# The rotary steps of a grouped attention: another DMA queue, later due times, a ranked read-out, and a wider last attention

## The chip, the cores and the metric

The kernel runs on one core of a Trainium2 chip. The metric is the device time of one execution in microseconds, as the median of three runs. Before the change it is 1803.03 us (1802.46 to 1805.33).

## The reference, cut to what matters

An encoder of two layers on 512 tokens plus 16 meta tokens (T = 528), width 2048, float32. Layer 0 is grouped-query attention, layer 1 is gated linear attention. The change touches layer 0 alone:

```
proj = rmsnorm(h) @ w_in                    # q: 16 heads x 128, k, v: 8 x 128, gate: 2048
q = axial_rope(rmsnorm(q, q_norm))          # per head; likewise k
x1, x2 = split(x, 2)                        # inside each half of 64 rows
rotate(x) = concat(x1*cos - x2*sin, x2*cos + x1*sin)
o = softmax(q k^T * 128**-0.5) v            # one k/v head serves two q heads
y = (o * silu(gate)) @ w_out
```

## The kernel before, in words

Every float32 operand is split into a high part and the rest (`split`, L128: a cast on ACT, a subtraction on DVE), and each product is three matmuls on PE. A projection (`project`, L156) computes 128 output columns for all tokens in two halves of 264. It walks 16 blocks of the contraction, so it has 2 x 16 x 3 = 96 matmuls. Its weights come in two units of 512 KB on SP's queue (`wraw`, two buffers) and are split into `whi` and `wlo` (three buffers).

Attention runs in eight groups g, each with one k head and two q heads. While PE attends in group g (`attention`, L656: nine query tiles, each with scores, a softmax on DVE and ACT, transposes, and then the product with v), it also projects k, q, q and v for group g+1 (`qkv`, L565, and `values`, L539). Nothing else fills PE in that time. In the last group, g = 7, it projects the gates 13, 14 and 15 instead; after that comes the output projection (`group`, L746).

The order of emission is kept by a planner. `Clock` counts planned microseconds: each three matmuls of a projection advance it by 3 x 271/2400 = 0.339, so a projection is 10.84. `clk.after(dt, fn)` emits `fn` when the count reaches its due time, and `clk.drive` steps through a generator whose yields are such times. `SLOTS[g]` is the planned distance of two query tiles. From the emitted program each engine's order of instructions is then fixed when the program is built: of the instructions whose inputs that builder expects to be there, the earliest in the program goes first, and an instruction inside `tc.high_priority(400)` counts as 400 places earlier. Work of a later program place can so come ahead of its place where the builder expects an engine to be free. On the chip each engine then runs its list strictly in order.

A rotation (`rope`, L290) is run for each of the 3 x 8 projected k and q tiles. ACT writes the scaled projection `qw` and its square `sq` (L286, L287). Four DMAs of 32 rows each copy `qw` to `qs` with neighbouring blocks of 32 rows exchanged (L294). `sq` is split into `sh` and `sl`. POOL multiplies `qw` by cos and `qs` by sin (L299, L300). At two due times after the projection, `sums` runs for the two halves: PE adds the squares over the 128 rows by a product with ones into the PSUM tile `ssq` (L304, L305), and DVE reads it out into `f` (L306). That PSUM tile comes from the pool `ps_o`, which has one buffer, and the product with v (`weighted`, L645, matmuls from L650) uses the same buffer. So PE can start the second `sums`, or a product with v, only after DVE's read-out of the `sums` before it. At a later due time `late` computes the reciprocal root on ACT (L133, L134), adds `qs` to `qw` (L310), multiplies by the root (L311) and splits the result into the q or k tiles.

For group 0 there is no projection ahead: `first_group` (L574) starts the three rotations 4.2 planned us apart and then waits before the first attention tile; meanwhile PE projects for group 1.

Of the kernel before, what the change touches and what calls it, by code (L numbers as in the profile page):

```python
# [14 lines left out]
ALU = mybir.AluOpType  # L15
# [4 lines left out]
P = 128  # L20
# [12 lines left out]
G_HEADS = 4  # L33
SCALE = 128 ** -0.5
AHEAD = 400
SLOTS = (3.0, 3.5, 3.8, 3.8, 3.8, 3.8, 3.8, 2.6)


class Clock:
# [43 lines left out]
def hybrid_encoder(  # L83
# [5 lines left out]
    nc = tc.nc  # L89
    V, A, G, PE = nc.vector, nc.scalar, nc.gpsimd, nc.tensor  # L90
    clk = Clock()
# [27 lines left out]
    def col(i):  # L119
        return cols[:, i:i + 1]  # L120
# [7 lines left out]
    def split(hi, lo, src):  # L128
        A.copy(hi, src)  # L129
        V.tensor_tensor(lo, src, hi.bitcast(F32), op=ALU.subtract)  # L130

    def rsqrt_inplace(t):
        A.activation(t, t, AF.Ln)  # L133
        A.activation(t, t, AF.Exp, scale=-0.5)  # L134
# [21 lines left out]
    def project(src, c0, parts, evac, last_k=None, ws=None):  # L156

        ws = ws or [weights(src[:, k0:k0 + 8, c0:c0 + P]) for k0 in (0, 8)]
        for a, b in parts:
            ps = ps_p.tile([P, 512], F32, tag="pp", name="pp")[:, :b - a]  # L160
            for k in range(KT):
                wh, wl = ws[k // 8]
                three(ps, wh[:, k % 8], wl[:, k % 8], k, a, b, k == 0, k == KT - 1)
                clk.step(3 * (b - a + 7) / 2400)
                if last_k and (a, b) == parts[-1]:
                    last_k(k)
            evac(ps, a, b)
# [109 lines left out]
    erow = c0.tile([P, T], F32, name="erow")  # L277
    rcol = c0.tile([P, 5], F32, name="rcol")
    def take(wcol):

        qws.append(qws.pop(0))
        qw = qws[-1]
        sq = wk.tile([P, T], F32, tag="sq", name="sq")

        def evac(ps, a, b):
            A.activation(qw[:, a:b], ps, AF.Copy, scale=wcol)  # L286
            A.activation(sq[:, a:b], ps, AF.Square)  # L287
        return qw, sq, evac

    def rope(qw, sq, outs, steps):  # L290
        qs = wk.tile([P, T], F32, tag="qs", name="qs")
        for b in range(4):
            s = b ^ 1
            nc.sync.dma_start(out=qs[b * 32:b * 32 + 32, :], in_=qw[s * 32:s * 32 + 32, :])  # L294
        sh = wk.tile([P, T], F32R, tag="sh", name="sh", bufs=1)
        sl = wk.tile([P, T], F32R, tag="sl", name="sl", bufs=1)
        split(sh, sl, sq)
        f = sq
        G.tensor_tensor(qw, qw, cos, op=ALU.mult)  # L299
        G.tensor_tensor(qs, qs, sin, op=ALU.mult)  # L300

        def sums(a, b):
            ps = ps_o.tile([P, 512], F32, tag="o", name="ssq")[:, :b - a]
            PE.matmul(ps, ones_r, sh[:, a:b], start=True, stop=False)  # L304
            PE.matmul(ps, ones_r, sl[:, a:b], start=False, stop=True)  # L305
            V.scalar_tensor_tensor(f[:, a:b], ps, 1.0 / P, erow[:, a:b], op0=ALU.mult, op1=ALU.add)  # L306

        def late():
            rsqrt_inplace(f)
            V.tensor_tensor(qw, qw, qs, op=ALU.add)  # L310
            V.tensor_tensor(qw, qw, f, op=ALU.mult)  # L311
            for hi, lo, a, b in outs:
                split(hi, lo, qw[:, a:b])
        for step, part in zip(steps, HALVES):
            clk.after(step, lambda part=part: sums(*part))
        clk.after(6.5, late)

    def qk_tiles(p, n):
        kh, kl = [p.tile([P, T], F32R, name=f"k{w}{n}") for w in "hl"]
# [59 lines left out]
    for i, (si, off) in enumerate(((0, 0), (1, 0), (1, P))):  # L379
        for j, (a, b) in enumerate(HALVES):  # L380
            n = 2 * i + j
            if n < 3:
                ps = ps_p.tile([P, 512], F32, tag="pp", name="pp")
            else:
                ps = ps_g.tile([P, 512], F32, name=f"g{n}")
            ps = ps[:, :b - a]
# [152 lines left out]
    def values(g):  # L539
        vh = wa.tile([P, 4, P], F32R, tag="vh", name="vh")  # L540
        vl = wa.tile([P, 4, P], F32R, tag="vl", name="vl")
        vm = vm_bufs[g % 2]
        if g:
            project(w_in0, 3072 + g * P, HALVES, lambda ps, a, b: A.copy(vt[:, a:b], ps))

        def late():
            ps = ps_t.tile([P, 512], F32, tag="t", name="vps")
            for t in range(4):
                PE.transpose(ps[:, t * P:(t + 1) * P], vt[:, t * P:(t + 1) * P], ident)
            for t in range(4):  # L550
                pst = ps[:, t * P:(t + 1) * P]
                A.activation(vh[:, t, :], pst, AF.Copy, scale=rcol[:, t:t + 1])
                V.scalar_tensor_tensor(vl[:, t, :], pst, rcol[:, t:t + 1], vh[:, t, :].bitcast(F32),
                                       op0=ALU.mult, op1=ALU.subtract)
            pm = ps_t.tile([P, 512], F32, tag="t", name="vpm")[:META, :P]
            PE.transpose(pm, vt[:, SEQ:T], ident)
            rm = rcol[:META, 4:5]
            A.activation(vm[0:META], pm, AF.Copy, scale=rm)
            A.activation(vm[64:64 + META], pm, AF.Copy, scale=rm)
            V.scalar_tensor_tensor(vm[32:32 + META], pm, rm, vm[0:META].bitcast(F32),  # L560
                                   op0=ALU.mult, op1=ALU.subtract)
        clk.after(1.2 if g else 2.0, late)
        return vh, vl, vm

    def qkv(g):  # L565
        qk, outs = qks[g % 2]
        vv = values(g) if g == 1 else None
        for i, c in enumerate((2048 + g * P, 2 * g * P, (2 * g + 1) * P)):
            qw, sq, evac = take(col(KN if i == 0 else QN))
            project(w_in0, c, HALVES, evac)  # L570
            rope(qw, sq, outs[i], (4.4, 5.6))
        return qk, vv or values(g)

    def first_group():  # L574
        for i in range(3):
            sq = wk.tile([P, T], F32, tag="sq", name="sq")
            A.activation(sq, qws[i], AF.Square)
            A.activation(qws[i], qws[i], AF.Copy, scale=col(QN if i else KN))
            rope(qws[i], sq, qks[0][1][i], (2.6, 3.9))
            yield 4.2 if i < 2 else 7.5  # L580

    def stored_gates(hs, held):

        grs = [wa.tile([P, T], F32, tag="gr", name="gr") for _ in hs]
        for gr, h in zip(grs, hs):
            nc.sync.dma_start(out=gr, in_=g_d[h])
        yield 6.0
        for gr, h in zip(grs, hs):
            yield 5.0
            V.tensor_tensor(gr, gr, rrow, op=ALU.mult)  # L590
            gs = silu(gr)
            yield 4.0
            og = held[h % 2]
            V.tensor_tensor(og, og, gs, op=ALU.mult)
            nc.gpsimd.dma_start(out=og_d[h], in_=og)
# [7 lines left out]
    def gate(h, last_k=None):  # L603
        gr = wa.tile([P, T], F32, tag="gr", name="gr", bufs=2)
        project(w_in0, 4096 + h * P, HALVES,
                lambda ps, a, b: V.tensor_tensor(gr[:, a:b], ps, rrow[:, a:b], op=ALU.mult), last_k)
        return silu(gr)
# [79 lines left out]
    def o_tiles():  # L687
        return [wa.tile([P, T], F32, tag="o", name="o_sb", bufs=4) for _ in range(2)]
# [3 lines left out]
    for g in range(KV):  # L692
        o_sb = o_tiles()
        att = attention(qk, vv, o_sb, SLOTS[g])
        lead = first_group() if g == 0 else iter([6.5] if g == 1 else [])
        att = clk.drive(chain(lead, att))
        gates = [] if g == 0 else [2 * g - 2, 2 * g - 1]
        stored = clk.drive(stored_gates([h for h in gates if h < 13], held))
        if g + 1 < KV:
            nxt = qkv(g + 1)  # L700
        for h in gates:
            if h < 13:
                continue
            gs = gate(h)
            og = held[h % 2]
            V.tensor_tensor(og, og, gs, op=ALU.mult)
            nc.gpsimd.dma_start(out=og_d[h], in_=og)
        if g + 1 < KV:
            clk.finish(att, stored)
            qk, vv = nxt  # L710
            held = o_sb
# [28 lines left out]
    for m in range(2):  # L740
        for j, (a, b) in enumerate(HALVES):
            ps = (ps_t.tile([P, 512], F32, tag="t", name="po") if m and j else
                  ps_p.tile([P, 512], F32, tag="pp", name="pp"))[:, :b - a]
# [75 lines left out]
    for i in range(2):  # L819
        for a, b in HALVES:  # L820
            ps = ps_g.tile([P, 512], F32, name=f"g{i}{a}")[:, :b - a]
# [109 lines left out]
    for a, b in HALVES:  # L931
        ps = ps_t.tile([P, 512], F32, tag="t", name="lrf")[:64, :b - a]
# [481 lines left out]
```

## Time and profile before

| | |
|---|---|
| median of three runs | 1803.03 us |
| profiled execution, its own time | 1801.33 us |
| its span, first to last instruction | 1799.6 us |
| mean granted TensorE clock | 0.997 |
| PE busy (matmuls) | 1758.1 us, 98% |
| DVE busy | 1128.4 us, 63% |
| ACT busy | 951.3 us, 53% |
| POOL busy | 208.3 us, 12% |

Busy times of PE are those of pipelined matmuls, so a gap counts only once the last matmul in flight has ended. DMA-issuing instructions are not counted as busy. The attention of layer 0 lies between about 205 and 757 us.

### The profile page before, as it was taken

The page shows a single profiled execution, that of the slowest core. Times are in us where ns is not written, and L with a number is a line of the kernel's source. Part 1 is how long each engine was busy: PE and PEld are TensorE (multiplying, and loading weights), DVE is VectorE, ACT ScalarE, POOL GpSimd, SP SyncE. Part 2 cuts the span into 40 slices and gives each one's busy share as a digit, 9 for nine tenths or more (in the row PEclk, how much of TensorE's full clock was granted, in tenths as well). Part 3 has the DMA queues.
Part 4 walks back from the last instruction along what each step waited for, and adds up shares of the span by engine and source line. Part 5 has one row for each costly group of instructions (what it writes and reads, how often), then busy time and mean ns, then how long its engine had stood idle before and what let it go on. Part 6 is the DMA issues. An engine that isn't in the chain of part 4 may idle for free.

```text
span 1799.6 us, 31638 instructions
## 1 busy us (share of the span) xinstructions
PE 1758.1 (98%) x12591; PEld 1654.9 (92%) x12591; DVE 1128.4 (63%) x1904; ACT 951.3 (53%) x1909; POOL 208.3 (12%) x270
## 2 busy tenths in 40 slices
PE   8999899999999999999999999999999999999998
PEld 8999899999999999999999899988898989888886
DVE  5877687666666666641238787667585765764224
ACT  5543465555565555543338544477685765863221
POOL 3000212111211111121111101110000100000000
PEclk9999999999999999999999999999999999999999
DMA  8444433233232323243336344343232332345333
GB/s 258 134 126 119 131 97 89 72 95 99 81 89 79 94 80 99 90 142 94 94 93 213 114 124 126 100 131 104 85 113 74 110 95 83 88 159 176 94 94 129
DMA packets 266788, 200.95 MB, mean 112 GB/s; under 512 B 9772, under 2 KB 239856, under 8 KB 266112
## 3 DMA queue, kind: packets, MB, share of 16 engines
q1 hardware_dynamic: 256496, 166.03, 32.2%
q0 software_dynamic: 10144, 32.90, 5.1%
q8 instruction: 99, 1.62, 0.4%
q14 instruction: 49, 0.40, 0.1%
HBM read 164.39 MB, written 28.01 MB: 107 GB/s over the span
## 4 chain that ended last, share of the span: by engine, by line
PE 81%; DVE 7%; ACT 4%; DMA 3%; issue 2%; POOL 2%; SPq 1%; DVEq 0%; POOLq 0%; ACTq 0%
PE pp L152 15%; PE pp L154 14%; PE pp L153 14%; PE pp L229 4%; PE pp L231 4%; PE pp L230 4%; PE f L1326 2%; PE f L1324 2%; PE f L1325 2%; DVE wlo L130 2%; DMA qs<-qw 1%; ACT whi L129 1%; PE pT L630 1%; PE o L1144 1%; PE o L1145 1%
## 5 line engine op out<-in xcount | busy, mean ns | idle before, releaser
L152 PE MATMUL pp<-uh,whi 128*128 128x264 f32 (+1 forms) x2320 | 712.6, 307 | 1.0 <-POOL whi L360 0.9
L154 PE MATMUL pp<-uh,wlo 128*128 128x264 f32 (+1 forms) x2320 | 702.8, 303 | 0.4 <-POOL wlo L361 0.3
L153 PE MATMUL pp<-ul,whi 128*128 128x264 f32 (+1 forms) x2320 | 703.0, 303 | 0.0
L130 DVE TENSOR_TENSOR wlo<-wraw,whi 128x1024 fp32r<-128x1024 f32 (+1 forms) x239 | 292.8, 1226 | 290.6 <-ACT whi L129 288.9
L154 PEld LDWEIGHTS pp<-uh,wlo 128*128 128x128 f32 x2320 | 437.6, 189 | 17.5 <-POOL wlo L361 0.6
L152 PEld LDWEIGHTS pp<-uh,whi 128*128 128x128 f32 x2320 | 437.6, 189 | 17.4 <-POOL whi L360 1.2
L153 PEld LDWEIGHTS pp<-ul,whi 128*128 128x128 f32 x2320 | 438.0, 189 | 13.9 <-DVE ul L422 0.4
L129 ACT CAST whi<-wraw 128x1024 fp32r<-128x1024 f32 (+1 forms) x239 | 248.9, 1042 | 279.8 <-PE pp L153 90.3
L129 ACT CAST whi<-x 128x1024 fp32r<-128x1024 f32 x48 | 50.1, 1046 | 70.4 <-PE pp L230 52.0
L620 ACT ACTIVATE pn<-s,mx 128x528 f32<-128x528 f32 (+1 forms) x72 | 50.5, 701 | 69.2 <-DVE mx L617 69.1
L1326 PE MATMUL f<-whi,ul 128*128 128x512 f32 x192 | 75.6, 394 | 0.0
L1324 PE MATMUL f<-whi,uh 128*128 128x512 f32 x192 | 75.5, 393 | 0.0
L1325 PE MATMUL f<-wlo,uh 128*128 128x512 f32 x192 | 75.3, 392 | 0.0
L231 PE MATMUL pp<-uh,wlo 128*128 128x264 f32 x264 | 75.2, 285 | 0.0
L229 PE MATMUL pp<-uh,whi 128*128 128x264 f32 x264 | 75.0, 284 | 0.0
L230 PE MATMUL pp<-ul,whi 128*128 128x264 f32 x264 | 74.7, 283 | 0.0
L130 DVE TENSOR_TENSOR wlo<-x,whi 128x1024 fp32r<-128x1024 f32 x48 | 58.6, 1223 | 23.2 <-ACT whi L129 23.2
L299 POOL TENSOR_TENSOR qw<-qw,cos 128x528 f32<-128x528 f32 x24 | 32.8, 1366 | 297.0 <-DMA qs<-qw 249.4
L635 DVE TENSOR_TENSOR pl<-pT,ph 128x512 fp32r<-128x512 f32 (+1 forms) x80 | 47.5, 594 | 28.1 <-ACT ph L634 27.3
L634 ACT CAST ph<-pT 128x512 fp32r<-128x512 f32 (+1 forms) x80 | 40.6, 508 | 40.7 <-PE pT L630 22.2
L617 DVE TENSOR_REDUCE mx<-s 128x1 f32<-128x528 f32 (+1 forms) x72 | 50.7, 704 | 14.6 <-PE s L614 13.2
L229 PE MATMUL pp<-th,whi 128*128 128x264 f32 x192 | 56.1, 292 | 0.4 <-ACT th L129 0.4
(402 smaller groups left out, 3703.2 us busy)
## 6 DMA issues: line engine op xcount, KB each, us to landing
wraw<-in_attn_w_in_dram SPq DMA_DIRECT2D x82, 512.0 KB, 4.3
wraw<-in_gla_w_in_dram SPq DMA_DIRECT2D x81, 512.0 KB, 3.9
wraw<-in_attn_w_out_dram SPq DMA_DIRECT2D x32, 512.0 KB, 3.8
wraw<-in_gla_w_out_dram SPq DMA_DIRECT2D x32, 512.0 KB, 3.8
x<-in_gla_w_in_dram SPq DMA_DIRECT2D x15, 512.0 KB, 4.5
qs<-qw SPq DMA_DIRECT2D x96, 66.0 KB, 2.6
x<-in_attn_w_in_dram SPq DMA_DIRECT2D x12, 512.0 KB, 4.4
x<-h_d SPq DMA_DIRECT2D x32, 132.0 KB, 3.6
```

The source lines that it names most:

```text
L129: A.copy(hi, src)
L130: V.tensor_tensor(lo, src, hi.bitcast(F32), op=ALU.subtract)
L152: PE.matmul(ps, wh, uh[:, k, a:b], start=first, stop=False)
L153: PE.matmul(ps, wh, ul[:, k, a:b], start=False, stop=False)
L154: PE.matmul(ps, wl, uh[:, k, a:b], start=False, stop=last)
L229: PE.matmul(ps, w[0][:, k], bh[:, k], start=k == 0, stop=False)
L230: PE.matmul(ps, w[0][:, k], bl[:, k], start=False, stop=False)
L231: PE.matmul(ps, w[1][:, k], bh[:, k], start=False, stop=k == KH - 1)
L617: V.reduce_max(mx, s, axis=AX.XY, negate=True)
L1324: PE.matmul(ps, uh[:, k, ts], wh[:, kk], start=(k == 0), stop=False)
L1325: PE.matmul(ps, uh[:, k, ts], wl[:, kk], start=False, stop=False)
L1326: PE.matmul(ps, ul[:, k, ts], wh[:, kk], start=False, stop=(k == KT - 1))
```

## The change

The 96 shifted copies are issued on ACT's queue instead of SP's. `late` is due 8.3 instead of 6.5 planned us after a rotation starts. The second `sums` of a rotation is due at 6.6 instead of 5.6, except in the first group. The read-out L306 is ranked 400 places earlier. In the first group the attention starts 9.0 instead of 7.5 after the third rotation, with a tile distance of 2.9 instead of 3.0; in group 1 it starts 8.5 instead of 6.5 after the group's start; in group 7 the tile distance is 3.1 instead of 2.6. The instructions and their shapes stay the same.

```diff
-SLOTS = (3.0, 3.5, 3.8, 3.8, 3.8, 3.8, 3.8, 2.6)
+SLOTS = (2.9, 3.5, 3.8, 3.8, 3.8, 3.8, 3.8, 3.1)
...
-            nc.sync.dma_start(out=qs[b * 32:b * 32 + 32, :], in_=qw[s * 32:s * 32 + 32, :])
+            nc.scalar.dma_start(out=qs[b * 32:b * 32 + 32, :], in_=qw[s * 32:s * 32 + 32, :])
...
-            V.scalar_tensor_tensor(f[:, a:b], ps, 1.0 / P, erow[:, a:b], op0=ALU.mult, op1=ALU.add)
+            with tc.high_priority(AHEAD):
+                V.scalar_tensor_tensor(f[:, a:b], ps, 1.0 / P, erow[:, a:b], op0=ALU.mult, op1=ALU.add)
...
-        clk.after(6.5, late)
+        clk.after(8.3, late)
...
-            rope(qw, sq, outs[i], (4.4, 5.6))
+            rope(qw, sq, outs[i], (4.4, 6.6))
...
-            yield 4.2 if i < 2 else 7.5
+            yield 4.2 if i < 2 else 9.0
...
-        lead = first_group() if g == 0 else iter([6.5] if g == 1 else [])
+        lead = first_group() if g == 0 else iter([8.5] if g == 1 else [])
```

## Rows read from the trace of the kernel before

**Rows 1.** Busy times in three stretches: start:end us, length, engines, granted clock, DMA.

```profile
205.00:305.00 100.00, 90.38 (x724) 88.58 (x723) 73.43 (x133) 60.27 (x130) 24.39 (x19) 0.98 0.37 107
305.00:704.00 399.00, 387.24 (x3171) 381.99 (x3171) 266.79 (x529) 222.76 (x504) 63.55 (x54) 1.00 0.31 87
704.00:757.00 53.00, 50.99 (x401) 49.40 (x401) 34.37 (x74) 26.93 (x63) 5.04 (x5) 0.97 0.25 80
```

**Rows 2.** Waits of PE, 205 to 305 us: total us, times, longest.

```profile
PE ssq L304 <- DVE sq L306: 7.1, 2, 5.5
PE s L612 <- ACT pn L620: 2.3, 2, 1.4
```

**Rows 3.** Timeline of DVE: start, us, engine, line, op, [idle before <-releaser].

```profile
220.77 1.79 DVE L310 TENSOR_TENSOR qw<-qw,qs 128x528 f32<-128x528 f32 x1 [4.33 <-POOL qs L300]
222.66 1.61 DVE L311 TENSOR_TENSOR qw<-qw,sq 128x528 f32<-128x528 f32 x1
224.20 0.42 DVE L306 SCALAR_TENSOR_TENSOR sq<-ssq,erow 128x264 f32<-128x264 f32 x1
```

**Rows 4.** Timeline of PE at the longest stall.

```profile
224.67 0.59 PE L304 MATMUL ssq<-sh,ones_r 128*128 128x264 f32 x1 [5.48 <-DVE sq L306]
```

**Rows 5.** Timeline of SP's queue ahead of that stall.

```profile
207.48 1.33 SPq L294 DMA_DIRECT2D qs<-qw  x1
212.92 0.37 SPq L147 DMA_DIRECT2D wraw<-in_attn_w_in_dram  x1
213.35 3.13 SPq L294 DMA_DIRECT2D qs<-qw  x5
```

**Rows 6.** Timeline of POOL ahead of that stall.

```profile
218.17 1.31 POOL L299 TENSOR_TENSOR qw<-qw,cos 128x528 f32<-128x528 f32 x1 [9.58 <-DMA qs<-qw]
220.70 1.29 POOL L299 TENSOR_TENSOR qw<-qw,cos 128x528 f32<-128x528 f32 x1
```

**Rows 7.** Busy times around the two drops of the granted clock.

```profile
224.00:228.00 4.00, 3.33 (x17) 3.33 (x18) 3.65 (x7) 3.66 (x6) 0.00 (x0) 0.57 0.07 17
228.00:262.00 34.00, 32.65 (x271) 32.34 (x270) 29.49 (x55) 24.14 (x53) 8.86 (x6) 1.00 0.33 93
732.00:737.00 5.00, 4.80 (x27) 4.51 (x28) 2.68 (x11) 1.03 (x5) 0.88 (x2) 0.66 0.28 108
```

**Rows 8.** Waits of PE, 305 to 704 us.

```profile
PE ssq L304 <- DVE sq L306: 5.7, 5, 1.8
PE o L650 <- DVE sq L306: 5.0, 4, 1.6
```

**Rows 9.** Timeline of DVE at the end of one group.

```profile
558.50 0.69 DVE L635 TENSOR_TENSOR pl<-pT,ph 128x512 fp32r<-128x512 f32 x1 [2.60 <-ACT ph L634]
559.54 0.43 DVE L306 SCALAR_TENSOR_TENSOR sq<-ssq,erow 128x264 f32<-128x264 f32 x1
562.73 0.71 DVE L590 TENSOR_TENSOR gr<-gr,rrow 128x528 f32<-128x528 f32 x1 [2.76 <-DMA gr<-g_d]
563.36 0.43 DVE L306 SCALAR_TENSOR_TENSOR sq<-ssq,erow 128x264 f32<-128x264 f32 x1
```

**Rows 10.** Waits of PE, 704 to 757 us.

```profile
PE pT L630 <- DVE pl L635: 1.8, 1, 1.8
```

**Rows 11.** Instructions on the tile qs: durations ns min/median/max, first and last start.

```profile
L294 SPq DMA_DIRECT2D qs<-qw x96: 507/584/1328, 204.1 to 691.8; - x96
L310 DVE TENSOR_TENSOR qw<-qw,qs x24: 693/708/1786, 220.8 to 698.1; 128x528 f32<-128x528 f32 x24
```

**Rows 12.** Timeline of DVE: the split of the squares in two rotations.

```profile
466.27 0.70 DVE L130 TENSOR_TENSOR sl<-sq,sh 128x528 fp32r<-128x528 f32 x1
554.57 0.71 DVE L130 TENSOR_TENSOR sl<-sq,sh 128x528 fp32r<-128x528 f32 x1
```

**Rows 13.** Timeline of PE: the first sum in those rotations.

```profile
469.15 0.28 PE L304 MATMUL ssq<-sh,ones_r 128*128 128x264 f32 x1
556.36 0.29 PE L304 MATMUL ssq<-sh,ones_r 128*128 128x264 f32 x1
```

**Rows 14.** Waits of all engines, 195 to 780 us.

```profile
DVE qw L310 <- POOL qs L300: 37.3, 18, 4.3
```

## The prediction

> **What bounds the kernel now.** I read the page's busy shares first: PE is busy for 98% of the span. No instruction of PE is removed, so the change can only gain where PE stands still or runs at the lower clock. Next I read the busy times by stretch [rows 1]. In the attention of layer 0, which holds every edit, PE is idle for 100 - 90.4 = 9.6 us in the first stretch, 399 - 387.2 = 11.8 us in the middle and 53 - 51.0 = 2.0 us in the last group: 23.4 us, 1.3% of the time. That is the ceiling, but for the clock. The waits of PE then give the names.
>
> In the first stretch PE waits 7.1 us, in two waits, for DVE's read-out of the sums of squares, and 2.3 us for the exponential that frees the scores' PSUM tile [rows 2]. In the middle it waits 5.7 us in five waits for the read-out before a second sum, and 5.0 us in four waits for the read-out before a product with v [rows 8]. In the last group one wait of 1.8 us is for DVE's subtraction behind a transpose [rows 10]. So 7.1 + 5.7 + 5.0 = 17.8 us of the 23.4 hang on one small DVE instruction (L306, 0.43 us).
>
> Last, the timelines show why that instruction is late. In the long stall PE starts again at 224.67 [rows 4] after a read-out at 224.20, which stood in DVE's list behind the rotation's L310 and L311. L310 had waited 4.33 us for POOL [rows 3], and POOL 9.58 us for the shifted copies [rows 6]. Those were held on SP's queue: one went out at 207.48, the next only behind a weight load at 212.92 [rows 5], whose buffer was not free earlier. At a group's end it is another chain: the first read-out, at 559.54, stands behind a subtraction that waited 2.60 us for ACT, and the second, at 563.36, behind a stored gate that waited 2.76 us for its own load [rows 9].
>
> The granted clock falls twice in the attention, to the 1.2 GHz level for part of each of two short stretches (mean 0.57 and 0.66), just after PE had stood still [rows 4, 7, 10]. At full clock a matmul costs 32.65/271 = 0.1205 us [rows 7]. So the 17 matmuls from 224 to 228 should have taken 2.05 us and took 3.33, a loss of 1.3; the 27 from 732 to 737 should have taken 3.25 and took 4.80, a loss of 1.55.
>
> **The change part by part.** The sum is made against the profiled execution (1801.33 us, of which 1.7 lie outside the span). The median of the runs is 1.7 us above it, and I carry that over by taking the gain off 1803.03.
>
> *First rotations.* On ACT's queue the copies of rotation 0 no longer stand behind the load of 212.92. They can go out right behind the activation that writes their source, around 204 to 207 instead of 204 to 214, and POOL's first multiplication comes some 9 us earlier (it waited 9.58). L310 then no longer holds DVE in front of the read-out, and `late`, due at 8.3, is emitted behind the second rotation's two sums (due at 6.8 and 8.1), where at 6.5 it was ahead of them. Two edits so remove the same stall: 5.5 us, and the clock's 1.3 behind it. The other wait of that row, 7.1 - 5.5 = 1.6, may stay, because DVE was then waiting for a weight load; I count half of it, 0.8. Sum: 5.5 + 1.3 + 0.8 = 7.6. Bounds: 0, and 7.1 + 1.3 + 2.3 = 10.7 if the wait for the exponential goes as well. What is late next is that exponential, and I leave its 2.3 us in.
>
> *Ends of groups.* The ranked read-out overtakes only what the builder expected to be ready at the same time. It does not overtake an instruction that was already ahead of it in the list because ACT or a load was expected earlier, and both waits of [rows 9] are of that kind. The wider distance of the two sums (2.2 planned us instead of 1.2) gives the first read-out 1.0 us more; four of the five waits are below or near that (5.7/5 = 1.1 on average). But the second sum moves 1.0 us closer to the product with v, which works against the 5.0. Bounds: 0 and 10.7. I take half, 5.3.
>
> *Last group.* At 3.1 a tile, its ten steps take 31 planned us instead of 26, beside 32.5 of projections (three of 10.84). The stretch is less dense, and the stall of 1.8 and the clock's 1.55 may go; the chain behind it (two gates at once on ACT, POOL and DVE) is not touched. Of 3.35 I take half, 1.7. Widening costs nothing as such: the last two heads are read only at step 14 of the output projection, 14 x 4 x 0.339 = 19 planned us after the gates. Without that cover it would cost the 5 planned us.
>
> *The copies on ACT.* This is the new cost. Ahead of the cast of the squares ACT now issues four DMAs per rotation. No row shows an issue on ACT; the nearest is the same DMA on SP, 0.584 us [rows 11]. So 4 x 0.584 = 2.34 us per rotation and 56 us in all, beside ACT's busy times of 60, 223 and 27 us in the three stretches [rows 1]. Behind them in ACT's list stand the cast of the squares, weight casts, exponentials and transposes' copies. What PE sees first is its first sum, which needs the split squares. In a typical rotation the split ended at 466.97 and PE came at 469.15, 2.18 us to spare; in a tight one 555.28 and 556.36, 1.08 to spare [rows 12, 13]. The issues overdraw these by 0.16 and 1.26. Over the 21 rotations after the first group that is 3.4 or 26 us, and 0 where the builder moves the sums on PE by the same amount. I take 3.0, near the typical row.
>
> *At nothing.* SP loses 96 issues: its weight loads may go a little earlier, but PE waited for none of them in this stage. `late` 1.8 later: for the second q head it now ends after the group's last projection has begun to run out (8.3 of 10.84), but that head is read only in the third tile. If that cover is gone, it costs at most 1.8 at each of 7 boundaries, 12.6. The starts of groups 0 and 1 (plans of 46.4 and 43.5 instead of 45.9 and 41.5, against 43.4 of projections) are hidden by the next group's projections, which need nothing of the attention; uncovered, 0.5 and 0.1.
>
> Sum: -7.6 - 5.3 - 1.7 + 3.0 = -11.6, so 1803.0 - 11.6 = 1791.4 us.
>
> **The rivals.**
>
> *Only the first stall goes.* The ends of groups keep their waits, since both of [rows 9] come from ACT and a load; the last group keeps its too. -7.6 + 3.0 = -4.6: 1798.4. For it: the ranked instruction has nothing to overtake there. Against it: the wider spacing of the sums holds whatever the order.
>
> *DVE collides with POOL instead of waiting for it.* DVE stood still for 37.3 us in 18 waits at L310 while POOL multiplied [rows 14]. With earlier copies and a later `late`, DVE does other work in that time. But where POOL ran beside it (220.70 to 221.99) L310 took 1.79 us instead of its median 0.708 [rows 3, 6, 11], 1.08 more. At 18 places that is 19.4 us of DVE. PE lost 17.8 us to L306 while DVE lost 37.3, so 19.4 x 17.8/37.3 = 9.3 come back to PE: -11.6 + 9.3 = -2.3, 1800.7. Against it: a split of a PSUM tile or a maximum may fall there just as well, and no row shows those slowed. The Trainium skill ("SBUF — State Buffer", section "Who interferes with whom") says that a DVE instruction with two SBUF inputs and a GpSimd instruction that reads SBUF block each other for a whole instruction; the stretched L310 agrees with that, and by that rule the collisions hit the additions, multiplications and weight splits alone.
>
> *ACT becomes late (the slower side).* The 2.34 us of issues push the cast of the squares, and PE's list keeps its place for the first sum, so every sum waits. It decides from 14.6/21 = 0.7 us per rotation on, where it eats all gains. Between the typical overdraft of 0.16 and the tight one of 1.26, with exponentials and copies of transposes pushed as well, 1.0 us is a fair bad case: 21 x 1.0 = 21, so -14.6 + 21 = +6.4, 1809.4. For it: ACT runs its list in order, and its work at a group's end was already late by 2.60. Against it: the builder knows the DMAs and can place the sums later.
>
> *All waits go.* 10.7 + 10.7 + 3.35 = 24.7 without a cost on ACT: 1778.3.
>
> **How the numbers follow.** A measurement tells about 0.2%, 3.6 us, from no change. The forecast has 0.50, with its own range from 1783 to 1799 (8 either way: the second term may come out at 0 or at 10.7, which is 5.3, and ACT's cost at 0 or 6). Only the first stall: 0.15, POOL collisions: 0.10, ACT late: 0.17, all waits: 0.08. Faster (below 1799.4): 0.48 + 0.11 + 0.02 + 0.08 = 0.69. Slower (above 1806.6): 0.14 of ACT's 0.17. Same: the rest, 0.17. The range from 1781 to 1806 leaves out the far part of "all waits" (0.05) and most of "ACT late" (0.13).
>
> **What would show it.** First stretch right: POOL's first multiplication near 209, no PE wait above 2 us there, the granted clock 1.00 from 224 to 228. Wrong: PE still waits for L306 there. Ends of groups: the sum of the two rows of L306 at 5 to 6 us instead of 10.7. ACT: waits of PE's L304 for the split squares are the cost; above 10 us in total the forecast is wrong. Last group: a granted clock of 1.00 from 704 to 757. POOL collisions would show as a median of L310 or L311 well above 0.71. The prediction as a whole is wrong if PE's idle time in the attention doesn't fall below 17 us.

## The result, and the profile after

The changed kernel takes 1811.88 us (median of seven runs, 1807.24 to 1814.7). The kernel before takes 1802.46 us in the runs beside it. The ratio is 1.0049, with a 95% interval of 1.0034 to 1.0064: slower by about 9 us, where 12 us less were predicted.

The page of the profile after begins with the span (1799.6 before) and the busy times:

```profile
span 1810.6 us, 31594 instructions
PE 1763.6 (97%) x12591; PEld 1660.6 (92%) x12591; DVE 1124.3 (62%) x1904; ACT 946.4 (52%) x1909; POOL 208.6 (12%) x270
```

The span grew by 11.0 us. PE's busy time grew by 5.5 with the same 12591 matmuls, so half of the loss is matmuls that took longer, and the other half, 5.5, is PE standing still. About 0.95 us of the 11.0 are already there in the first 40 us, where nothing was changed. The difference then builds up in steps through the attention: at the 2000th matmul PE is 1.7 us behind the kernel before, at the 3000th 3.0, at the 4000th 6.6, at the 5000th 8.2, at the 5500th 11.2, and at the 6000th 10.1. After that it stays within a microsecond of that.

The same three stretches as in [rows 1]; the last is five us longer here:

```profile
205.00:305.00 100.00, 89.72 (x713) 87.56 (x711) 69.28 (x126) 57.82 (x125) 24.91 (x21) 0.98 0.37 107
305.00:704.00 399.00, 385.05 (x3128) 379.75 (x3129) 263.81 (x533) 218.35 (x503) 61.11 (x52) 0.99 0.31 88
704.00:762.00 58.00, 54.59 (x422) 53.58 (x421) 36.61 (x76) 28.79 (x67) 7.72 (x7) 0.94 0.23 72
```

PE's idle time is 10.3 + 13.9 + 3.4 = 27.6 us; it was 23.4. The prediction wanted it below 17.

The waits of PE in the first stretch, against [rows 2] (from L306 on, lines have moved down by one):

```profile
PE pT L631 <- DVE pl L636: 3.0, 1, 3.0
PE ssq L305 <- DVE sl L130: 2.3, 1, 2.3
PE ssq L304 <- DVE sq L307: 1.7, 1, 1.7
PE ssq L304 <- ACT sh L129: 1.2, 1, 1.2
```

The stall of 5.5 us is gone, and four waits of 1.2 to 3.0 us have taken its place. In the middle stretch, the two rows of the read-out, against [rows 8]:

```profile
PE o L651 <- DVE sq L307: 7.7, 4, 3.2
PE ssq L304 <- DVE sq L307: 2.0, 5, 0.6
```

The wait before the second sum fell from 5.7 to 2.0 us. The wait before the product with v rose from 5.0 to 7.7, and its longest from 1.6 to 3.2. In the last group, against [rows 10], that wait appears anew:

```profile
PE o L651 <- DVE sq L307: 2.1, 1, 2.1
PE pT L631 <- DVE pl L636: 1.3, 2, 1.2
```

The granted clock falls to the 1.2 GHz level for part of five short stretches instead of two [rows 7]; columns as there:

```profile
224.00:228.00 4.00, 4.00 (x21) 3.87 (x21) 3.74 (x6) 3.28 (x5) 0.37 (x1) 0.57 0.08 20
306.00:310.00 4.00, 4.00 (x24) 4.00 (x23) 3.06 (x8) 1.63 (x5) 0.00 (x0) 0.57 0.77 238
497.00:501.00 4.00, 3.13 (x15) 3.16 (x16) 2.52 (x5) 1.90 (x3) 0.00 (x0) 0.57 0.22 68
709.00:713.00 4.00, 4.00 (x20) 4.00 (x21) 1.40 (x2) 2.20 (x4) 0.00 (x0) 0.58 0.00 0
743.00:747.00 4.00, 4.00 (x23) 4.00 (x22) 1.44 (x6) 0.65 (x3) 0.30 (x1) 0.57 0.17 68
```

At 0.1205 us a matmul [rows 7] their 103 matmuls should have been busy for 12.4 us and were for 19.1: a loss of 6.7, against 1.3 + 1.55 = 2.85 before. So 3.9 us of the 5.5 more that PE was busy are the clock's. With 4.2 us more idle time that is 8.1 of the 9.1 us by which these two executions drift apart in the attention (10.1 less the 0.95 from the start); the medians differ by 9.4.

One of the five shows how it comes about. DVE at the end of the group at 490 us:

```profile
489.59 0.71 DVE L130 TENSOR_TENSOR sl<-sq,sh 128x528 fp32r<-128x528 f32 x1 [2.13 <-ACT sh L129]
494.89 2.37 DVE L311 TENSOR_TENSOR qw<-qw,qs 128x528 f32<-128x528 f32 x1 [2.58 <-POOL qs L300]
497.29 0.43 DVE L307 SCALAR_TENSOR_TENSOR sq<-ssq,erow 128x264 f32<-128x264 f32 x1
```

POOL, and then PE, at the same place:

```profile
492.25 1.32 POOL L299 TENSOR_TENSOR qw<-qw,cos 128x528 f32<-128x528 f32 x1 [14.70 <-DMA qs<-qw]
493.52 1.33 POOL L300 TENSOR_TENSOR qs<-qs,sin 128x528 f32<-128x528 f32 x1
495.38 1.31 POOL L601 TENSOR_TENSOR gs<-gs,gr 128x528 f32<-128x528 f32 x1
```

```profile
493.14 0.28 PE L304 MATMUL ssq<-sh,ones_r 128*128 128x264 f32 x1
497.87 0.57 PE L651 MATMUL o<-ph,vh 128*128 128x272 f32 x1 [3.23 <-DVE sq L307]
```

PE has begun the sum at 493.14, but the read-out comes only at 497.29. Ahead of it in DVE's list stands the rotation's addition (L311), which waits 2.58 us for POOL and then takes 2.37 instead of 0.71 while POOL works on the gate (L601). PE stands still for 3.23 us, and behind that the clock falls (497 to 501). At the other four waits of PE before a product with v, the addition stands directly ahead of the read-out as well, after waits of 2.4 to 3.7 us for POOL.

How often this is so can be counted in the trace: in 10 of 24 rotations before, and in 22 of 24 after, the addition stands ahead of the second read-out in DVE's order. From the second sum to its read-out it takes 1.21 us before (median of the 21 later rotations), 2.16 us after. PE doesn't pay at every such place: it waits only where it needs the buffer before the read-out has come. In the kernel before, the addition is directly ahead at one of the four waits before a product with v; at the other three it is a stored gate that waits for its load, as in [rows 9].

### The profile page after: what moved, and what is told of

Its sections match the earlier page's. It is cut to its first block, busy times and chain, and to the rows that moved or that the text cites. A ratio compares the mean times of both kernels' runs of the same rounds, so it can differ in the third digit from the quotient of the medians.

```text
span 1810.6 us, 31594 instructions
## 1 busy us (share of the span) xinstructions
PE 1763.6 (97%) x12591; PEld 1660.6 (92%) x12591; DVE 1124.3 (62%) x1904; ACT 946.4 (52%) x1909; POOL 208.6 (12%) x270
## 4 chain that ended last, share of the span: by engine, by line
PE 53%; DVE 3%; ACT 2%; DMA 1%; issue 1%; POOL 0%; ACTq 0%; DVEq 0%; POOLq 0%; SPq 0%
PE pp L152 10%; PE pp L154 10%; PE pp L153 9%; PE f L1327 2%; PE f L1325 2%; PE f L1326 2%; PE pp L229 2%; PE pp L230 2%; PE pp L231 2%; PE o L1145 1%; PE o L1146 1%; PE o L1144 1%; PE pp L1327 1%; PE pp L1325 1%; PE pp L1326 1%
## 5 line engine op out<-in xcount | busy, mean ns | idle before, releaser
L230 PE MATMUL pp<-tl,whi 128*128 128x264 f32 x192 | 54.6, 285 | 0.0
L231 PE MATMUL pp<-th,wlo 128*128 128x264 f32 x192 | 54.4, 284 | 0.0
```

Of the source, the lines that this page charges most:

```text
L230: PE.matmul(ps, w[0][:, k], bl[:, k], start=False, stop=False)
L231: PE.matmul(ps, w[1][:, k], bh[:, k], start=False, stop=k == KH - 1)
```

## The experiments

The expectations name these theories: A, the queue's (ACT, stopped by four issues, casts the squares late); B, the spacing's (the second sum comes close to the product with v); and B2, the order of addition and read-out, which was thought of only after the first two groups of runs. All ratios are against the kernel before on the same chip, with their 95% interval. Four chips were used, on which the kernel before has medians of 1800.6 to 1802.7 us, so runs on different chips compare better by their ratios.

**The parts.** First the change without its queue, and the queue by itself.

```diff
-            nc.scalar.dma_start(out=qs[b * 32:b * 32 + 32, :], in_=qw[s * 32:s * 32 + 32, :])
+            nc.sync.dma_start(out=qs[b * 32:b * 32 + 32, :], in_=qw[s * 32:s * 32 + 32, :])
```

> All edits, but the shifted copies stay on SP's queue. Theory A (the four issues stand on ACT ahead of the cast of the squares, 0.602 us each in the trace of after, so the split squares come 2.3 us later): the loss of 9 us goes, 1804 or less, and the cast follows the projection's last activation within 0.9 us again. Rival B (the second sum, due 1.0 planned us nearer to the product with v, makes PE wait for its read-out: 9.8 us of waits before the products instead of 5.0, and the clock drops that follow): 1809 to 1812, and the waits before the products stay near 9.8.

Measured 1807.93, 1.0040 (1.0028 to 1.0052), between the two ranges. It is still slower without ACT's queue, so within the change that queue isn't the main cause. Its waits of PE from 195 to 780 us:

```profile
PE o L651 <- DVE sq L307: 11.2, 5, 2.8
PE ssq L304 <- DVE sq L307: 6.4, 2, 4.9
```

The kernel before with that one line on `nc.scalar`:

> The kernel before with only the copies moved to ACT's queue. Theory A: 1809 to 1814. Rival B: within 3 us of before, 1800 to 1806, with PE's waits before the products with v near 5.0 us.

Measured 1827.47, 1.0140 (1.0123 to 1.0157): +25 us, outside what either theory gave. On ACT the four issues hold up what stands behind them:

```profile
474.11 2.44 ACTq L294 DMA_DIRECT2D qs<-qw  x4
476.59 0.63 ACT L129 CAST sh<-sq 128x528 fp32r<-128x528 f32 x1 [2.29 <-DMA qs<-qw]
```

PE waits 17.7 us for the read-out before a second sum and 8.3 us before a product with v (195 to 780 us). What stands ahead of the late read-outs is again the rotation's own addition. DVE, and then PE, at one of them:

```profile
459.79 0.71 DVE L310 TENSOR_TENSOR qw<-qw,qs 128x528 f32<-128x528 f32 x1 [3.17 <-POOL qs L300]
460.52 0.70 DVE L617 TENSOR_REDUCE mx<-s 32x1 f32<-32x528 f32 x1
461.15 0.41 DVE L306 SCALAR_TENSOR_TENSOR sq<-ssq,erow 128x264 f32<-128x264 f32 x1
```

```profile
461.61 0.58 PE L304 MATMUL ssq<-sh,ones_r 128*128 128x264 f32 x1 [2.04 <-DVE sq L306]
```

It is so at 12 of the 13 waits for a read-out above 0.3 us, 24.1 of their 25.2 us, and the addition is ahead of the second read-out in 18 of 24 rotations. So the trace points to the order here too, and not to the late cast alone; this kernel wasn't run with another order, so how the 25 us divide isn't shown. The queue costs 25 us alone, and 2 to 4 within the change (1.6 by the ratios 1.0049 and 1.0040, whose intervals overlap; 4.0 by the medians 1811.88 and 1807.93).

All edits, but the second sum back at 5.6:

> All edits, but the second sum is due at 5.6 again. Theory A: 1810 to 1814, as after. Rival B: the 4.8 us more of waits before the products and two or three drops of the clock of about 1.4 us each go, 1803 to 1807.

Measured 1827.88, 1.0140 (1.0125 to 1.0156). Both theories were wrong: with ACT's queue, the later second sum makes up for most of the queue's cost, about 16 us. Here the addition is ahead of the second read-out in 16 of 24 rotations. That the sums need the 1.0 us because the cast is late was not tested.

All edits without the rank (`tc.high_priority`):

> All edits, but the read-out of the sums has its ordinary rank. Theories A and B alike: within 2 us of after, 1810 to 1814, since the instructions that hold DVE (the addition that waits for POOL) are ahead of the read-out in either order. If the rank itself does harm, by pulling the read-out ahead of work that PE waits for, it is 1808 or less.

Measured 1812.32, 1.0063 (1.0051 to 1.0076): not to be told from the change (1.0034 to 1.0064), and the addition is ahead in 22 of 24 rotations with the rank or without it. No effect of the rank shows.

**The due times alone.** The kernel before with the second sum at 6.6 and `late` at 6.7:

```diff
-        clk.after(6.5, late)
+        clk.after(6.7, late)
...
-            rope(qw, sq, outs[i], (4.4, 5.6))
+            rope(qw, sq, outs[i], (4.4, 6.6))
```

> The kernel before with only the second sum at 6.6 instead of 5.6, and the last step at 6.7 instead of 6.5, so that it stays behind the sum that it reads. Theory B (without the queue's delay the second read-out comes too close to the product with v): this edit carries the 7 us that the change still loses with the copies on SP; 1805 to 1809, the waits before the products near 11 us instead of 5.0, the waits before second sums about 5 us less. Rival (the later last step carries them): within 2 us of before, 1799 to 1803.

Measured 1811.34, 1.0044 (1.0032 to 1.0057), above the range of B: two numbers do as much harm as the whole change. The waits, 195 to 780 us, and DVE at a group's end:

```profile
PE o L650 <- DVE sq L306: 14.6, 6, 3.1
PE ssq L304 <- DVE sq L306: 6.8, 2, 5.5
```

```profile
496.64 0.71 DVE L310 TENSOR_TENSOR qw<-qw,qs 128x528 f32<-128x528 f32 x1 [1.19 <-POOL qs L300]
497.27 0.43 DVE L306 SCALAR_TENSOR_TENSOR sq<-ssq,erow 128x264 f32<-128x264 f32 x1
```

The addition is ahead of the read-out again, in 20 of 24 rotations. At two of the five long waits before a product with v (1.9 us and more) a stored gate that waits for its load stands ahead of the addition in turn; at three the addition itself waits for POOL. ACT's queue has no part in it.

`late` at 8.3 with the two later starts (9.0 and 8.5), the second sum left at 5.6:

> The kernel before with only the last step at 8.3 and the starts of attention in groups 0 and 1 at 9.0 and 8.5. Theory B: within 2 us of before, 1799 to 1803, or up to 5 us faster if the first stretch loses its long stall. Rival (the later last step collides with the next group's start): 1804 to 1809.

Measured 1805.61, 1.0012 (1.0003 to 1.0021): 2 to 3 us slower, inside the rival's range. In its profile only 0.9 us of that arise between the 1500th and the 6000th matmul, which is the attention; the addition is ahead in 9 of 24. A later `late` alone moves little.

**Is it the late cast?** After the change the cast of the squares follows ACT's last activation by 2.29 us (median), before by 0.03. Here the split is emitted ahead of the copies:

```diff
-        for b in range(4):
-            s = b ^ 1
-            nc.scalar.dma_start(out=qs[b * 32:b * 32 + 32, :], in_=qw[s * 32:s * 32 + 32, :])
...
         split(sh, sl, sq)
+        for b in range(4):
+            s = b ^ 1
+            nc.scalar.dma_start(out=qs[b * 32:b * 32 + 32, :], in_=qw[s * 32:s * 32 + 32, :])
```

> All edits, and the split of the squares is emitted ahead of the four copies, so that ACT casts before it issues. Theory A in its narrow form (PE's sum is late because the cast stands behind 2.4 us of issues): 4 to 8 us faster than after, 1804 to 1808, and the cast again within 1 us of the projection's last activation. Theory A in its wide form (ACT is late for everything, whatever comes first): within 2 us of after.

Measured 1813.45, 1.0051 (1.0037 to 1.0065): no gain, though the cast now comes after 0.35 us (median). The waits before the product with v are 12.4 us. In the full change the late cast isn't what costs; the addition is still ahead in 22 of 24. That ACT is late for everything would give the same time, but with no copies on ACT at all 1807.93 remain.

**Is it the addition?** First it was taken off DVE, in the kernel before and in the change:

```diff
-            V.tensor_tensor(qw, qw, qs, op=ALU.add)
+            G.tensor_tensor(qw, qw, qs, op=ALU.add)
```

> The kernel before, with the addition of the two products moved from DVE to POOL, so that no instruction of DVE waits for POOL ahead of a read-out (the multiplication behind it needs both read-outs anyway). If the addition is what holds DVE before the read-outs: PE's waits for the read-outs fall from 17.8 us to below 8 and the time to 1788 to 1795. If they come from ACT and from the stored gates' loads: 1797 to 1802. POOL gets 24 times 1.3 us more, beside 5 to 25% busy in this stage.

Measured 1802.23, 0.9993 (0.9984 to 1.0001): no gain for the kernel before. Its waits before the product with v fall to 2.8 us (195 to 780 us); those before the second sum are 12.2, as they were (12.8).

> All edits, and the addition of the two products on POOL instead of DVE, so that DVE holds nothing that waits for POOL ahead of the second read-out. Theory B2 (the later second sum is harmful because its read-out has slipped behind that addition, which waits for the copies and POOL): PE's waits before the products with v fall from 9.8 us to below 5 and the time to 1801 to 1807. Rival (the second sum itself is too near to the product with v, whatever stands ahead of the read-out): 1809 to 1814, waits as in after.

Measured 1802.77, 1.0007 (0.9997 to 1.0017): the loss of the change is gone. Other waits of PE are now the longest, 195 to 780 us:

```profile
PE s L613 <- ACT pn L621: 5.6, 4, 4.3
PE pTm L633 <- DVE vl L554: 5.5, 3, 2.6
```

Then the addition stayed on DVE, and its order alone was changed: it is kept behind its own rotation's second read-out in DVE's list.

```diff
+        read = [None]
...
-                V.scalar_tensor_tensor(f[:, a:b], ps, 1.0 / P, erow[:, a:b], op0=ALU.mult, op1=ALU.add)
+                read[0] = V.scalar_tensor_tensor(f[:, a:b], ps, 1.0 / P, erow[:, a:b], op0=ALU.mult, op1=ALU.add)
...
-            V.tensor_tensor(qw, qw, qs, op=ALU.add)
+            with tc.issue_after(read[0].ins):
+                V.tensor_tensor(qw, qw, qs, op=ALU.add)
```

> All edits, and the addition stays on DVE but is held in its list behind the second read-out of its own rotation. Theory B2: as the run with the addition on POOL, 1801 to 1807, the read-out within 1 us of the second sum. Rival: 1809 to 1814.

Measured 1794.99, 0.9967 (0.9956 to 0.9978): 17 us less than the change, and faster than before; more than expected. DVE at the same group's end, and the waits of PE, 195 to 780 us:

```profile
490.56 0.43 DVE L309 SCALAR_TENSOR_TENSOR sq<-ssq,erow 128x264 f32<-128x264 f32 x1 [1.47 <-PE ssq L307]
491.03 0.71 DVE L314 TENSOR_TENSOR qw<-qw,qs 128x528 f32<-128x528 f32 x1
```

```profile
PE pTm L636 <- DVE vl L557: 4.3, 2, 2.5
PE s L616 <- ACT pn L624: 4.1, 2, 3.8
PE ssq L306 <- DVE sq L309: 0.5, 1, 0.5
```

No wait for a read-out before a product with v is listed any more. The read-out follows its sum after 0.82 us (median). By its page PE is busy for 1757.9 us, 5.7 less than after the change with the same matmuls. So this order makes the loss: with the second sum as near to the product with v as in the change, the loss is gone.

The same hold in the kernel before:

> The kernel before, with the addition held behind the second read-out of its own rotation and nothing else. If the addition is the cause in before too, the 5.0 us of waits before the products go, and the time is 1794 to 1798; if before does not pay for it (its second sum at 5.6 comes ahead of the addition anyway, and its waits come from ACT and the gates' loads): 1799 to 1803.

Measured 1796.93, 0.9974 (0.9964 to 0.9984). The hold gains 5 us in the kernel before too. Its waits before the product with v fall from 5.0 to 2.3 us (1.3 of the 5.0 stood behind the addition); those before the second sum (11.9) stay. The rest of the 5 us isn't accounted for. With the hold in both kernels the change is no longer slower than the kernel before: 0.9967 (0.9956 to 0.9978) and 0.9974 (0.9964 to 0.9984).

**What ACT's queue is worth, and where.** The change with the copies on SP and the addition held:

> All edits with the copies on SP, and the addition held behind the second read-out. Theory B2: against the run with the copies on SP (1807.9) at least 8 us faster, 1794 to 1800, with PE's waits before the products below 3 us instead of 11.2. If the ACT queue is of use by itself, this is slower than the same with the copies on ACT (1795.0), by the long stall of the first stretch, 5 us: 1798 to 1801; if it is of harm, faster: 1788 to 1793.

Measured 1793.19, 0.9947 (0.9935 to 0.9959), below the range of B2 and next to that of a harmful queue: with the addition held, all copies on SP are 2 us (medians) to 4 us (ratios) faster than all on ACT, though the intervals touch.

The kernel before with ACT's queue in the first group alone, and the wide last attention:

```diff
-    def rope(qw, sq, outs, steps):
+    def rope(qw, sq, outs, steps, queue=nc.sync):
...
-            rope(qws[i], sq, qks[0][1][i], (2.6, 3.9))
+            rope(qws[i], sq, qks[0][1][i], (2.6, 3.9), nc.scalar)
```

> The kernel before with the copies on ACT's queue in the first group alone, and the last attention at 3.1. If the first stretch and the last group gained as the parts of the prediction had it (5 us in the run with the queue alone, 1 to 3 us in the runs with the wide last attention) and nothing else moves: 1794 to 1798. Rival (each such edit reshuffles the order behind it, and the gain is given back): 1800 to 1805.

Measured 1796.89, 0.9970 (0.9960 to 0.9980). So two parts of the change do gain, without the others.

The same kernel, with the addition on POOL except in the first group:

> As the run before this one, and the addition on POOL for all rotations but the first group's. With the addition on POOL alone the stretch from 328 to 705 us was 5 us shorter and the first 3 to 4 us longer; so here 1789 to 1795. Rival as there: 1799 to 1805.

Measured 1795.77, 0.9971 (0.9959 to 0.9984), and with the addition held instead:

> The kernel before with the copies on ACT in the first group alone, the last attention at 3.1, and the addition held behind the second read-out. If the parts add: the 1796.9 of that run without the hold, less the 3.3 us of waits before the products that it still had: 1792 to 1795. If the order is reshuffled and the gain given back: 1795 to 1800.

Measured 1794.86, 0.9959 (0.9947 to 0.9971). The first misses its range by 0.8 us. Both stand within 2 us of that kernel without them. In its trace no wait above 0.3 us for a read-out stands behind the addition, so there was little for them to gain. The hold was put into four kernels and gained in each, by the ratios 15 us in the change (17 by the medians), 17 in the change with copies on SP, 5 in the kernel before and 2 here.

Last, all edits, the addition held, ACT's queue in the first group and SP's in the others:

> All edits with the addition held behind the second read-out, and the copies on ACT in the first group alone. If the late cast of the squares is the only harm of the ACT queue and the first stretch its only use, this is the fastest: 1788 to 1793. Rival (with the addition out of the way the queue does not matter): 1793 to 1798.

Measured **1789.49, 0.9931 (0.9918 to 0.9943)**: the fastest, 13 us below the kernel before and 22 below the change. The three stretches (the last one is 46 us long here):

```profile
205.00:305.00 100.00, 93.00 (x731) 90.60 (x731) 72.73 (x132) 59.69 (x128) 25.15 (x19) 0.97 0.38 111
305.00:704.00 399.00, 394.21 (x3256) 391.51 (x3255) 274.78 (x549) 230.22 (x519) 64.32 (x54) 1.00 0.32 91
704.00:750.00 46.00, 44.62 (x366) 43.81 (x365) 33.71 (x66) 27.03 (x60) 5.14 (x5) 1.00 0.28 91
```

PE's idle time is 7.0 + 4.8 + 1.4 = 13.2 us, 10.2 below the kernel before, and from 305 us on the clock is full. Against the kernel with all copies on ACT and the addition held (1794.99), ACT's queue in the later groups costs 5.5 us. Against the one with all on SP (1793.19), ACT's queue in the first group gains 3.7 by the medians, but the intervals overlap, and of the 3.3 us between the two profiles 1.7 are there before the 500th matmul, where the kernels are alike. So that gain isn't clear of noise.

## Why the prediction was wrong

**The step that failed is "ends of groups"**: -5.3, with bounds of 0 and 10.7. These bounds left out a loss, although the step named where it would come (the second sum "moves 1.0 us closer to the product with v"). It took the nearer second sum as something that could eat the gain at most. By its own test, the two rows of L306 "at 5 to 6 us", it came to 2.0 + 7.7 = 9.7 in the middle stretch, with 2.1 more in the last group and three more drops of the clock. From the 3000th to the 5500th matmul (391 to 705 us before) the change fell back from 3.0 to 11.2 us, 8.2 us lost where this step and the copies together had a gain of 2.3. The first half of the step held: the waits before the second sum fell by 3.7. What it missed is DVE's order. With the copies on SP and the second sum at 5.6, the second read-out stands behind its rotation's addition in 9 to 11 of 24 rotations; at 6.6 in 20 or 22, on either queue, and so, at every long wait of the change, behind POOL. That `late` is due 1.8 later did not prevent it: the addition is emitted after the read-out and still comes ahead of it. The chain of [rows 9], where a gate's load holds the read-out, was rightly read for the kernel before, but the change put another one in its place. The prediction had read a stall of this kind in the first group, behind the addition of the rotation before [rows 3], and treated it as the first group's own. Two runs settle it: the spacing alone makes the loss (1.0044), and the order alone takes it away (0.9967 instead of 1.0049).

The prediction also summed this step and the copies as separate terms, and they aren't separate. Alone, the later second sum costs 8 us and the queue 25; together, with the other edits, they cost 9. Going from SP to ACT at 6.6 costs 2 to 4 us; going from 5.6 to 6.6 on ACT gains 16.

**First rotations** (-7.6) mostly failed too. POOL's first multiplication was to start near 209; it starts at 214.82, against 218.17 in the kernel before [rows 6]. The first three copies did go out at once, but the fourth met on ACT what it was to escape on SP:

```profile
205.83 1.86 ACTq L294 DMA_DIRECT2D qs<-qw  x3
212.07 1.05 ACT L129 CAST whi<-wraw 128x1024 fp32r<-128x1024 f32 x1 [5.21 <-DMA wraw<-in_attn_w_in_dram]
212.08 0.51 ACTq L294 DMA_DIRECT2D qs<-qw  x1
```

It is issued at 212.08, behind a weight cast that waited 5.21 us for its load; on SP the remaining copies went out from 213.35 [rows 5]. The stall of 5.5 us went, but waits of 8.2 us in all stand in the stretch, PE is idle there for 10.3 us instead of 9.6, and the clock still falls at 224 us. In the best kernel the same copies are as late (POOL starts at 214.25), and ACT's queue in the first group is worth 3.7 us at most, half of the term.

**The copies on ACT** (+3.0, bounds 0 and 26) were about right in size within the change: 2 to 4 us, and 5.5 where the addition is held and the first group keeps ACT's queue. Alone they cost 25, near the upper bound. The bounds held; which end is met depends on the second sum's due time, which the step had not linked to it. What it priced, the first sum waiting for a late cast, is not what the waits of the queue alone show: they stand behind the addition. Waits of PE for the split squares were to show the cost, above 10 us if the forecast was wrong; from 195 to 780 us they come to 1.2 and 2.3 us, both in the first stretch. The cost within the change did not show there.

**The last group** (-1.7) half held: from the 5500th to the 6000th matmul the change makes up 1.1 us, with PE idle for 1.5 us instead of 2.0. The clock's 1.55 stayed: it falls at 743 us as it did at 732. All kernels with the wide last attention make up 1.0 to 1.2 us there where that drop stays, and 2.3 to 2.7 where it does not come (the change with copies on SP 2.7); the five without the width make up nothing (0.0 to -0.3). The sign in the profile did not come: the granted clock from 704 us on is 0.94.

**The rivals.** "ACT becomes late" gave 1809.4 and is nearest to the time, but its mechanism isn't this one: with the cast early again the change stays at 1813.45, and with no copies on ACT at 1807.93. "DVE collides with POOL" appears at single places: the 2.37 us above and one addition of 1.81 at 296 us, against a median of 0.709 for all 24. By the Trainium skill ("SBUF — State Buffer", section "Who interferes with whom") a DVE instruction with two SBUF inputs and one of GpSimd that reads SBUF block each other. Those two rows agree, but two other additions, at 424 and 568 us, kept 0.71 though POOL began a multiplication 0.5 us after their start, as it did at 494.89. "At nothing" for the later `late` and starts is off by 2 to 3 us (1.0012, and the interval begins at 1.0003).

**Still open.** About 1 of the 9.1 us isn't accounted for by idle time and clock. Why the addition on POOL gains nothing in the kernel before, though it takes 2.2 us of waits away, isn't settled: in its profile it loses 2.1 us from the 1500th to the 2000th matmul and makes up 3.6 by the 5500th. Every edit rearranges the lists of all engines, so differences of 2 or 3 us between two kernels needn't be the edit's own. The number of rotations with the addition ahead doesn't give the size of a loss: 22 go with 9 us, 18 with 25. Whether the addition's order makes the 25 us of the queue alone is read from its waits, not tried.

## What to carry to other kernels

When a due time is moved, list what then stands ahead of the moved instruction on its engine, above all ahead of a short read-out that frees the only buffer PE can go on with; an instruction there that itself waits for another engine passes its whole wait on. A rank or a later emission need not change such an order; tying the waiting instruction behind the read-out does: 15 to 17 us here. Four DMAs issued from ACT held its next instruction up by 2.3 us a rotation, and with the addition held ACT's queue in the later groups still cost 5.5 us, so move only those copies whose own queue holds them up. And when two edits act on the same wait, don't add their prices: 8 and 25 us made 9 here.

## What the runs showed of the hardware that had not been expected

An issue on ACT takes as long as on SP (medians of 602 and 584 ns), and ACT's next instruction comes only after the four of them; the copies also land later. On the tile qs, after the change (before: [rows 11], and a median of 2.6 us from issue to landing):

```profile
L294 ACTq DMA_DIRECT2D qs<-qw x96: 514/602/1714, 205.8 to 700.6; - x96
L311 DVE TENSOR_TENSOR qw<-qw,qs x24: 701/709/2370, 217.5 to 707.7; 128x528 f32<-128x528 f32 x24
DMA to landing us min/median/max: 1.9/3.9/6.3
```

Landing takes 3.9 us instead of 2.6; it is 3.8 to 4.0 in all seven kernels with all copies on ACT and 2.3 to 3.0 in the seven with all on SP. POOL's second product ends 8.50 us after the projection's last activation (median of the later rotations) against 8.53 before, and against 7.66 in the change with copies on SP: the other queue made nothing earlier there.

How long PE stood still did not by itself decide on the clock. Ahead of the five drops PE's last gaps were 2.3, 2.6, 3.2, 2.1 and 1.2 us. The longest gap but one, 3.04 us up to 256.89, was followed by a full clock:

```profile
257.00:261.00 4.00, 4.00 (x33) 3.73 (x33) 3.10 (x9) 2.21 (x6) 0.00 (x0) 1.00 0.00 0
```

Each drop cost 1.1 to 1.6 us of matmul time, so the gap of 3.2 us at 497 cost some 4.5 in all. What tells these gaps apart, no run here shows.
